# The second MLP projection's first 512 columns by seven block products in place of eight

## The chip, the cores and the metric

The kernel runs on one core of a Trainium2 chip. The metric is the device time of one execution in microseconds; what is compared is the median of several runs. The time before is 2069.7 us, the median of 3 runs (2069.42 to 2069.75).

## What is computed

A trunk of two layers on 256 tokens of width 2048. Each layer has a mixing half (RMSNorm, one input projection, attention heads and gated groups, an output projection, a residual add) and an MLP half. The change lies in the MLP, whose reference is:

```python
D_MODEL = 2048; SEQ = 256; DEPTH = 2
D_FF = 4 * D_MODEL
for l in range(DEPTH):
    ...
    h2 = rms_norm(x, norm2_g[l])
    x = x + jnp.square(jax.nn.relu(h2 @ w_up[l])) @ w_down[l]
return rms_norm(x, final_g)
```

## The kernel before

**Number format.** All weights and activations are float32. TensorE works in a reduced format (float32r), so each operand is split in two: ScalarE (ACT) writes the high part as a rounded copy (`hi` of a weight, L122), VectorE (DVE) writes the low part, the operand minus its high part (`lo`, L132). Every product is then three matmuls: high by high, high by low, low by high (L293, L295, L297). Activations are kept split in the same way: `hs` for the normed input, `half` for the hidden tensor (`to_half`, L494 to L496).

**Pieces of weight.** All weights stream through once, in pieces of 512 KB (class `Sub`: 128 partitions by 1024). One piece feeds one *step*. In a column-major step (`transposed`, L265) the piece holds 4 tiles of 128 rows by 256 columns; the weights are the stationary operand, and the 256 tokens move: 24 matmuls of 128x256. In a token-major step (`natural`, L300), used for parts of the input projection, 128 tokens are the stationary operand and 512 weight columns move. A piece has 6 buffers for the raw data, 7 for `hi` and 6 for `lo` (L47 to L49).

**The order.** It is written out by the last loop (L666 to L686), one step at a time: the `hi` of the piece five steps ahead, the `lo` of the piece four steps ahead, the DMA of the next raw piece, the step's matmuls, then what follows the step. Each engine takes its own instructions strictly in that order. Small jobs go through a queue (`later`, `run_queue`, L151 and L164): at the end of a step, jobs that are due are issued until a budget of 1.2 is used up (L52), each job with a written-down cost.

**The MLP.** The hidden width of 8192 is cut in eighths of 1024. The loop at L605 issues, for each eighth, 16 steps of `w_up` (four quarters of 256 hidden rows, four steps each), then 16 steps of `w_down` for the eighth before. After each quarter `after_up` (L594) scales the sums on DVE (L599), applies the squared ReLU on DVE (L600), and splits the result (ACT L495, DVE L496). After every second `w_down` step `update` (L351) adds 256 rows' sums into `x` (DVE L356). In the last eighth the update is final: in the first layer it is followed by the next layer's `hs` (ACT L193, DVE L197) and the squares for the norm (ACT L206, DVE L210), in the last layer by the squares and the gain (L206, L210, L214).

**PSUM.** Four banks (`acc`) serve the steps in turn, four (`aux`) the small matmuls.

## Time and profile before

| | |
|---|---|
| median of 3 runs | 2069.7 us |
| the profiled execution's own time | 2068.91 us |
| its span, first to last instruction | 2067.1 us |
| granted TensorE clock over the span | 0.998 |
| busy share of TensorE, VectorE, ScalarE | 99%, 61%, 45% |
| matmul instructions | 17242 |
| read from HBM | 390.65 MB, 190 GB/s over the span |

A row of the groups gives the line and engine, the operation, output and inputs, the shape, how often; then the busy time in all, the mean of one in ns, and the idle time of that engine just before. A row of the timeline gives start and length in us, and in square brackets how long the engine had been idle and what ended it. In the timeline a merged row (x4) runs from the start of the first to the end of the last. Matmuls overlap, so their spacing is read from their starts.

### The profile page before, as it was taken

The numbers are of one execution on the slowest core, as the hardware profiler recorded it, in microseconds if no ns is written. First come the engines' busy times: TensorE is split into PE (matmuls) and PEld (weight loads), VectorE is DVE, ScalarE is ACT, GpSimd is POOL, SyncE is SP. The second block draws the span as 40 slices with busy tenths as digits, with TensorE's granted clock in tenths as the row PEclk, the third lists the DMA queues.
The fourth block names the chain that finished last, engine by engine and source line by source line (L and its number), as shares of the span: only waits on it lengthen the run. The fifth ranks groups of instructions, "written<-read, shape, count | busy, mean of one in ns | idle before, by whom it ended". The sixth has DMA issues, their size and how long they took to land.

```text
span 2067.1 us, 40218 instructions
## 1 busy us (share of the span) xinstructions
PE 2054.5 (99%) x17242; PEld 2018.3 (98%) x17242; DVE 1253.6 (61%) x1494; ACT 933.0 (45%) x1135; POOL 67.8 (3%) x90
## 2 busy tenths in 40 slices
PE   9999999999999999999999999999999999999997
PEld 7998999999999999999989989999999999999997
DVE  7666766556555655655756666665565555555655
ACT  7555444344343443434545654543444434434434
POOL 0002300000000000000000032000000000000000
PEclk9999999999999999999999999999999999999999
DMA  8545555555555555555564455555655656555562
GB/s 318 183 164 178 189 192 183 197 202 186 189 200 201 187 188 198 201 188 201 186 216 160 169 186 181 194 182 204 204 184 184 204 194 200 190 192 196 187 201 91
DMA packets 112115, 395.37 MB, mean 191 GB/s; under 512 B 12352, under 2 KB 16448, under 8 KB 111936
## 3 DMA queue, kind: packets, MB, share of 16 engines
q1 hardware_dynamic: 110800, 389.86, 55.4%
q8 instruction: 135, 2.21, 0.4%
q10 hardware_dynamic: 1136, 2.94, 0.4%
q14 instruction: 44, 0.36, 0.1%
HBM read 390.65 MB, written 2.10 MB: 190 GB/s over the span
## 4 chain that ended last, share of the span: by engine, by line
PE 99%; DVE 0%; DMA 0%; ACT 0%; issue 0%; ACTq 0%; DVEq 0%
PE acc L293 29%; PE acc L297 29%; PE acc L295 29%; PE acc L316 3%; PE acc L318 3%; PE acc L317 3%; PE aux L541 0%; PE aux L443 0%; PE aux L485 0%; PE aux L472 0%; DVE x L696 0%; DMA x<-in_xT 0%; PE aux L446 0%; PE aux L487 0%; PE aux L384 0%; PE aux L221 0%
## 5 line engine op out<-in xcount | busy, mean ns | idle before, releaser
L122 ACT ACTIVATE hi<-raw 128x1024 fp32r<-128x1024 f32 (+1 forms) x741 | 755.6, 1049 | 453.3 <-PE acc L297 374.9
L132 DVE TENSOR_TENSOR lo<-raw,hi 128x1024 fp32r<-128x1024 f32 (+1 forms) x741 | 864.5, 1213 | 52.3 <-ACT hi L122 24.1
L293 PE MATMUL acc<-hs,hi 128*128 128x256 f32 x2816 | 779.8, 277 | 0.0
L297 PE MATMUL acc<-hs,hi 128*128 128x256 f32 x2816 | 777.4, 276 | 0.0
L295 PE MATMUL acc<-hs,lo 128*128 128x256 f32 x2816 | 777.4, 276 | 0.0
L293 PE MATMUL acc<-half,hi 128*128 128x256 f32 x2560 | 706.7, 276 | 0.0
L297 PE MATMUL acc<-half,hi 128*128 128x256 f32 x2560 | 706.6, 276 | 0.0
L295 PE MATMUL acc<-half,lo 128*128 128x256 f32 x2560 | 706.6, 276 | 0.0
L295 PEld LDWEIGHTS acc<-hs,lo 128*128 128x128 f32 x2816 | 528.7, 188 | 0.4 <-issue 0.2
L293 PEld LDWEIGHTS acc<-hs,hi 128*128 128x128 f32 x2816 | 528.6, 188 | 0.4 <-issue 0.2
L297 PEld LDWEIGHTS acc<-hs,hi 128*128 128x128 f32 x2816 | 528.5, 188 | 0.0
L295 PEld LDWEIGHTS acc<-half,lo 128*128 128x128 f32 x2560 | 480.5, 188 | 0.0
L293 PEld LDWEIGHTS acc<-half,hi 128*128 128x128 f32 x2560 | 480.5, 188 | 0.0
L297 PEld LDWEIGHTS acc<-half,hi 128*128 128x128 f32 x2560 | 480.5, 188 | 0.0
L356 DVE TENSOR_TENSOR x<-x,acc 128x512 f32<-128x512 f32 (+1 forms) x145 | 99.2, 684 | 318.8 <-PE acc L297 318.8
L495 ACT ACTIVATE half<-mz 128x512 fp32r<-128x512 f32 x64 | 40.6, 634 | 363.7 <-DVE mz L600 363.7
L599 DVE TENSOR_TENSOR mz<-acc,nR 128x512 f32<-128x512 f32 x64 | 44.3, 692 | 230.1 <-PE acc L297 230.1
L316 PE MATMUL acc<-hi,hs 128*128 128x512 f32 x256 | 101.6, 397 | 0.8 <-ACT hs L193 0.8
L318 PE MATMUL acc<-hi,hs 128*128 128x512 f32 x256 | 100.7, 393 | 0.0
L317 PE MATMUL acc<-lo,hs 128*128 128x512 f32 x256 | 99.9, 390 | 0.0
L193 ACT ACTIVATE hs<-x,cols 128x256 fp32r<-128x256 f32 x64 | 29.0, 501 | 96.0 <-DVE x L356 94.8
L496 DVE TENSOR_TENSOR half<-mz,half 128x512 fp32r<-128x512 f32 x64 | 44.3, 692 | 44.8 <-ACT half L495 44.8
(99 smaller groups left out, 688.8 us busy)
## 6 DMA issues: line engine op xcount, KB each, us to landing
raw<-in_w SPq DMA_DIRECT2D x731, 512.0 KB, 4.3
raw<-in_w SPq DMA_DIRECT2D x10, 256.0 KB, 5.3
x<-in_xT SPq DMA_DIRECT2D x7, 256.0 KB, 5.6
out<-x SPq DMA_DIRECT2D x7, 256.0 KB, 2.9
spb<-in_b_sp ACTq DMA_DIRECT2D x2, 512.0 KB, 8.2
wsp<-in_w_sp ACTq DMA_DIRECT2D x2, 512.0 KB, 9.7
con<-in_consts ACTq DMA_DIRECT2D x1, 512.0 KB, 7.5
x<-in_xT ACTq DMA_DIRECT2D x1, 256.0 KB, 4.2
```

The costliest lines, as they stand in the source:

```text
L122: act.activation(self.h[:, j * m:(j + 1) * m], self.raw[:, j * m:(j + 1) * m], AF.Copy)
L132: vec.tensor_tensor(lo[:, r], self.raw[:, r], self.h[:, r].bitcast(F32), op=OP.subtract)
L293: pe.matmul(o, lhsT=hi, rhs=xs[:, 0, :], start=(k0 + k == 0 and (two or cb == 0)), stop=False, skip_group_check=True)
L295: pe.matmul(o, lhsT=wt.lo[:, k, cb * P:(cb + 1) * P], rhs=xs[:, 0, :], start=False, stop=False, skip_group_check=True)
L297: pe.matmul(o, lhsT=hi, rhs=xs[:, 1, :], start=False, stop=last, skip_group_check=True)
L316: pe.matmul(ps, lhsT=xh, rhs=hi, start=(k0 + k == 0), stop=False)
L317: pe.matmul(ps, lhsT=xh, rhs=lo, start=False, stop=False)
L318: pe.matmul(ps, lhsT=xl, rhs=hi, start=False, stop=(k0 + k == KC - 1))
L356: vec.tensor_tensor(xj, xj, ps[j][:, 0:S] if alone else pair(ps)[:, j, :], op=OP.add)
L495: act.activation(t[:, c:c + 2, 0, :], src, AF.Copy)
L496: vec.tensor_tensor(t[:, c:c + 2, 1, :], src, t[:, c:c + 2, 0, :].bitcast(F32), op=OP.subtract)
L599: vec.tensor_tensor(z, pair(ps), n2.R[:, None, :].to_broadcast([P, 2, S]), op=OP.mult)
```

## The change

The first 512 of the 2048 columns of `w_down` (constant `FAST`) are computed by Strassen's scheme in Winograd's form. The hidden eighth A (256 tokens by 1024) is cut in 2 by 2 blocks, and so is the weight block B (1024 by 512). Seven products of blocks, with sums of blocks as operands, replace the eight of the plain method. The other 1536 columns are computed as before, by 12 steps per eighth.

**Product groups.** Per eighth there are two steps of a new kind (`fast`), called product groups below. Each covers 2 of the 4 tiles of 128 rows in each row half of B. Its 7 products have 2 row tiles each and 3 matmuls per tile: 42 matmuls of 128x256, with tokens stationary (from `half` or from the new tile of sums, `shared`) and weight columns moving. A product group takes four entries in the list of pieces: `Top` and `Bottom` are loaded; two `Sums` are made in place in the raw buffers by two DVE subtractions each, and then split like any piece. Of `Top` only the left half is split.

```diff
+    class Top(Sub):
+        def high(self, parts):
...
+            act.activation(self.hi, self.left(), AF.Copy)
+        def low(self, parts):
...
+            vec.tensor_tensor(self.lo, self.left(), self.hi.bitcast(F32), op=OP.subtract)
...
+    class Sums(Sub):
+        loads = False
...
+        def high(self, parts):
+            t, b = self.top, self.bottom
+            if self.second:
+                vec.tensor_tensor(b.right(), b.right(), t.left(), op=OP.subtract)
+                vec.tensor_tensor(b.left(), b.right(), b.left(), op=OP.subtract)
+            else:
+                vec.tensor_tensor(t.left(), t.right(), t.left(), op=OP.subtract)
+                vec.tensor_tensor(t.right(), b.right(), t.right(), op=OP.subtract)
+            self.raw = (b if self.second else t).raw
+            Sub.high(self, 1)
...
+                if first and p == 0:
+                    banks.extend(aux_bank() for _ in range(4))
+                half = tiles[0][0]
+                sums_ready()
+                extra = sum_parts[0]
...
+                for n, (a, lower_rows, tt, b, cols) in enumerate((
+                        (half, 0, 0, top, left), (half, 1, 0, bottom, left), (extra, 1, 0, bottom, right),
+                        (extra, 1, 1, upper, left), (extra, 0, 1, upper, right),
+                        (extra, 0, 0, lower, right), (half, 1, 1, lower, left))):
+                    o = banks[n // 2][:, n % 2 * 256:n % 2 * 256 + 256]
+                    for k in range(2):
+                        xh, xl = (a[:, 4 * lower_rows + 2 * p + k, i, tt * P:(tt + 1) * P] for i in range(2))
...
```

**Sums of the hidden tensor.** `after_up` now writes its result into one tile for the whole eighth (`inner`, part of `ar`). After the last quarter a queued job adds the blocks in place (`sums`, four DVE instructions), and four more queued jobs split them into `shared` (`parts`, one ACT and one DVE instruction each). A product group's matmuls are issued only after all four (`sums_ready`).

```diff
+                if c == 768:
+                    summed[0] = False
...
+                    later(1, 1.5, sums)
...
+        def sums():
+            a11, a12, a21, a22 = (inner[:, 4 * k:4 * k + 4, t * P:(t + 1) * P] for t in range(2) for k in range(2))
+            vec.tensor_tensor(a22, a21, a22, op=OP.add)
+            vec.tensor_tensor(a21, a11, a21, op=OP.subtract)
+            vec.tensor_tensor(a11, a22, a11, op=OP.subtract)
+            vec.tensor_tensor(a12, a12, a11, op=OP.subtract)
+            def parts(k):
+                to_half(sum_parts[0], k, inner[:, k:k + 2, :])
+                summed[0] = k == 6
+            for k in range(0, 8, 2):
+                later(0, 1.2, lambda k=k: parts(k))
```

**Sums over the eighths.** The seven products stay in the four `aux` banks over all eight eighths of a layer. After the last product group they are combined (`combine`: one ACT copy, seven DVE instructions of 128x256), turned back to column-major by eight TensorE transposes (`turn_back`), and added into `x` by two more updates.

```diff
+        def combine():
+            p1, p2, p3, p5, p7, p6, p4 = (banks[n // 2][:, n % 2 * 256:n % 2 * 256 + 256] for n in range(7))
+            b1, u, c11, c12, c21, c22 = (blocks[:, n, :] for n in range(6))
+            act.activation(b1, p1, AF.Copy)
+            vec.tensor_tensor(u, b1, p6, op=OP.add)
...
+            later(1, 1.5, lambda: turn_back(0, c11, c21))
+            later(1, 1.5, lambda: turn_back(2, c12, c22))
+        def turn_back(c, first, second):
+            ps = aux_bank()
+            for j in range(2):
+                for tt, src in enumerate((first, second)):
+                    o = j * S + tt * P
+                    pe.transpose(ps[:, o:o + P], src[:, j * P:(j + 1) * P], ident)
+            later(0, 1.5, lambda: update(n3, c, ps, True, last))
```

**Order of the steps.** The two product groups of an eighth stand among the 16 `w_up` steps of the next eighth (after the fourth and the eighth); after the last eighth's `w_up` they stand among its 12 `w_down` steps (after the third and the sixth).

```diff
+            rest = up or down
+            n = len(quick) + 1
+            for i in range(n):
+                steps.extend(rest[len(rest) * i // (n + 1):len(rest) * (i + 1) // (n + 1)] if quick else rest)
+                steps.extend(quick[i:i + 1])
```

**Memory and loads.** Ten small tiles of the mixing half, which had buffers of their own, become slices of two tiles (`shared`, `ar`), whose space serves the sums in the MLP. The DMA of a raw piece is issued as a buffer is counted free (`load_more`); a product group's two raw buffers are counted free when its two sums have been split.

Three places where instructions move are shown from the lists of instructions. First VectorE at the start of a layer's second eighth. `lo` is a weight's low part, `ar` the hidden tensor or its sums, `half` and `shared` the split tensors. Before, behind the last quarter of the first eighth:

```order
L599 TENSOR_TENSOR mz_4646<-acc_4531,nR_3856 128x512
L600 SCALAR_TENSOR_TENSOR mz_4646<-mz_4646 128x512
L496 TENSOR_TENSOR half_4393<-mz_4646,half_4393 128x2x256
L132 TENSOR_TENSOR lo_4653<-raw_4464,hi_4616 128x1024
L132 TENSOR_TENSOR lo_4684<-raw_4494,hi_4651 128x1024
L132 TENSOR_TENSOR lo_4714<-raw_4529,hi_4682 128x1024
L132 TENSOR_TENSOR lo_4744<-raw_4560,hi_4712 128x1024
```

Four low parts stood there for the four steps up to the next quarter. Now, behind the same quarter's L715, L716 and L612 (the former L599, L600, L496):

```order
L175 TENSOR_TENSOR lo_4225<-raw_4037,hi_4188 128x512
L729 TENSOR_TENSOR ar_78<-ar_78 128x4x128
L730 TENSOR_TENSOR ar_78<-ar_78 128x4x128
L731 TENSOR_TENSOR ar_78<-ar_78 128x4x128
L732 TENSOR_TENSOR ar_78<-ar_78 128x4x128
L205 TENSOR_TENSOR raw_4037<-raw_4037 128x2x256
L206 TENSOR_TENSOR raw_4037<-raw_4067,raw_4037 128x2x256
L162 TENSOR_TENSOR lo_4260<-raw_4067,hi_4223 128x1024
L612 TENSOR_TENSOR shared_4222<-ar_78,shared_4222 128x2x256
L202 TENSOR_TENSOR raw_4067<-raw_4067,raw_4037 128x2x256
L203 TENSOR_TENSOR raw_4067<-raw_4067 128x2x256
L162 TENSOR_TENSOR lo_4292<-raw_4037,hi_4258 128x1024
```

The sums of the hidden tensor (L729 to L732), the sums of weights (L205, L206, L202, L203) and the first split sum (L612 into `shared`) have come in between the low parts of the first product group. The same list goes on with:

```order
L612 TENSOR_TENSOR shared_4222<-ar_78,shared_4222 128x2x256
L162 TENSOR_TENSOR lo_4324<-raw_4067,hi_4290 128x1024
L715 TENSOR_TENSOR ar_78<-acc_4227,nR_3810 128x512
L716 SCALAR_TENSOR_TENSOR ar_78<-ar_78 128x512
L612 TENSOR_TENSOR half_4352<-ar_78,half_4352 128x2x256
L612 TENSOR_TENSOR shared_4222<-ar_78,shared_4222 128x2x256
```

The third split sum (the last row) stands behind the next quarter (L715, which waits for the fourth step's matmuls), and the fourth one low part further on. In the later eighths all four stand among the `w_down` steps that come first.

Second, TensorE in that first product group, from its second product on (`aux` are the banks of the products):

```order
L408 MATMUL aux_4365<-hi_4223,half_3842 128x256
L410 MATMUL aux_4365<-lo_4260,half_3842 128x256
L411 MATMUL aux_4365<-hi_4223,half_3842 128x256
L408 MATMUL aux_4366<-hi_4223,shared_4222 128x256
L410 MATMUL aux_4366<-lo_4260,shared_4222 128x256
L411 MATMUL aux_4366<-hi_4223,shared_4222 128x256
```

The third product is the first that reads the sums; with row half 1 it needs the third of the four split sums, the high part at L408 and the low part at L411.

Third, VectorE in the first layer's last eighth, behind the second product group: the low parts of the next pieces, then `combine`:

```order
L162 TENSOR_TENSOR lo_11686<-raw_11461,hi_11630 128x1024
L162 TENSOR_TENSOR lo_11688<-raw_11523,hi_11678 128x1024
L162 TENSOR_TENSOR lo_11690<-raw_11525,hi_11680 128x1024
L162 TENSOR_TENSOR lo_11692<-raw_11565,hi_11682 128x1024
L745 TENSOR_TENSOR ar_78<-ar_78,aux_4367 128x256
L746 TENSOR_TENSOR ar_78<-ar_78,aux_4365 128x256
L747 TENSOR_TENSOR ar_78<-ar_78,aux_4367 128x256
L748 TENSOR_TENSOR ar_78<-ar_78,aux_4366 128x256
L749 TENSOR_TENSOR ar_78<-ar_78,aux_4366 128x256
L750 TENSOR_TENSOR ar_78<-ar_78,aux_4368 128x256
L751 TENSOR_TENSOR ar_78<-ar_78,aux_4366 128x256
```

TensorE has two `w_down` steps between the second product group and the first four transposes; the transposes' first pair needs L746 and L750. All of this is new; before, only two low parts and an update stood there per two steps.

More of the change, by code (lines that the diff above doesn't have):

```diff
@@ L52 @@
 BUDGET = 1.2
+FAST = 512
 WARM = 11
@@ L263, in trunk, with sums_ready, collect @@
     steps = []
+    summed, sum_parts = [True], [None]
+    def sums_ready():
+        run_until(lambda: summed[0])
+    def collect(fn, *args, **kw):
+        n = len(steps)
+        fn(*args, **kw)
+        part = steps[n:]
+        del steps[n:]
+        return part
     def transposed(name, l, row0, nk, col0, ncols, moving, after, between=None, apart=False):
@@ L608, in layer @@
             if e:
-                transposed("w_down", l, (e - 1) * 1024, 8, 0, D, from_tiles([hid[e - 1]], NH),
-                           lambda c, ps, e=e: update(n3, c // P, ps, e == 8, last), apart=last and e == 8)
+                down = collect(transposed, "w_down", l, (e - 1) * 1024, 8, FAST, D - FAST, from_tiles([hid[e - 1]], NH),
+                               lambda c, ps, e=e: update(n3, (c + FAST) // P, ps, e == 8, last), apart=last and e == 8)
+                quick = collect(fast, "w_down", l, (e - 1) * 1024, 0, [hid[e - 1]], banks, e == 1, e == 8,
+                                lambda: later(1, 1.5, combine))
@@ L611, in layer @@
+            rest = up or down
[3 more added lines that the diff above has]
+                steps.extend(quick[i:i + 1])
+            if quick:
+                steps.extend(rest[len(rest) * n // (n + 1):])
+            if up:
+                steps.extend(down)
         if last:
@@ L624, in trunk, with load_more @@
         layer(l, norms[2 * l], norms[2 * l + 1], norms[2 * l + 2], l == DEPTH - 1)
-    subs = [wt for wt, _, _ in steps if wt is not None]
-    n_load, n_high, n_low = [0], [0], [0]
+    subs = [u for wt, _, _ in steps if wt is not None for u in (wt if isinstance(wt, tuple) else (wt,))]
+    n_load, n_high, n_low, n_raw = [0], [0], [0], [0]
     xv = xT.rearrange("(k p) t -> p k t", p=P)
-    def load_to(n, parts=1):
-        while n_load[0] < min(n, len(subs)):
+    def load_more():
+        while n_load[0] < len(subs):
+            if not subs[n_load[0]].loads:
+                n_load[0] += 1
+                continue
+            if n_raw[0] == RAW_BUFS:
+                return
             c = 2 * n_load[0]
@@ L636, in load_to @@
                 nc.sync.dma_start(x[:, c:c + 2, :], xv[:, c:c + 2, :])
-            subs[n_load[0]].load(parts)
+            subs[n_load[0]].load(2 if n_load[0] < HALVES else 1)
             n_load[0] += 1
+            n_raw[0] += 1
     def high_to(n, parts=1):
         while n_high[0] < min(n, len(subs)):
+            if not subs[n_high[0]].loads:
+                low_to(n_high[0] - 1)
             subs[n_high[0]].high(parts)
@@ L657, in trunk @@
         pe.matmul(spare[:, 0:P], lhsT=ones, rhs=ones, start=True, stop=True)
-    for i in range(RAW_BUFS):
-        load_to(i + 1, 2 if i < HALVES else 1)
+    load_more()
     for i in range(2):
@@ L663, in trunk @@
     n_high[0] = n_low[0] = 2
+    n_raw[0] -= 2
     done = 0
```

68 lines of the change are left out of this document (63 added, 5 removed).

## The prediction

> **What bounds the kernel now.** I read the engines' busy shares first, then the chain that ended last, then TensorE's own waits, and the mean over a stretch of MLP.
>
> ```profile
> PE 2054.5 (99%) x17242; PEld 2018.3 (98%) x17242; DVE 1253.6 (61%) x1494; ACT 933.0 (45%) x1135; POOL 67.8 (3%) x90
> PE 99%; DVE 0%; DMA 0%; ACT 0%; issue 0%; ACTq 0%; DVEq 0%
> PE aux L229 <- DVE nr L255: 1.2, 1, 1.2
> PE acc L316 <- ACT hs L193: 0.8, 1, 0.8
> 340.00:700.00 360.00, 360.00 (x3178) 360.00 (x3177) 212.13 (x226) 147.57 (x154) 0.00 (x0) 1.00 0.57 195
> ```
>
> TensorE runs without a gap: the chain is its own instructions, and its listed waits inside the run are about 1 us. In the MLP it starts 3178 matmuls in 360 us, one each 0.1133 us, at full clock. VectorE has 212 of 360 us of work there, DMA 57%. So a matmul less is 0.1133 us less, as long as VectorE's part is ready in time. VectorE goes in order, and its lead decides:
>
> ```profile
> 377.45 0.69 DVE L599 TENSOR_TENSOR mz<-acc,nR 128x512 f32<-128x512 f32 x1 [3.53 <-PE acc L297]
> 378.17 0.69 DVE L600 SCALAR_TENSOR_TENSOR mz<-mz 128x512 f32<-128x512 f32 x1
> 379.57 0.69 DVE L496 TENSOR_TENSOR half<-mz,half 128x512 fp32r<-128x512 f32 x1 [0.70 <-ACT half L495]
> 380.18 4.62 DVE L132 TENSOR_TENSOR lo<-raw,hi 128x1024 fp32r<-128x1024 f32 x4
> 388.33 0.69 DVE L599 TENSOR_TENSOR mz<-acc,nR 128x512 f32<-128x512 f32 x1 [3.53 <-PE acc L297]
> 378.90 0.64 ACT L495 ACTIVATE half<-mz 128x512 fp32r<-128x512 f32 x1 [5.78 <-DVE mz L600]
> 379.44 2.94 ACT L122 ACTIVATE hi<-raw 128x1024 fp32r<-128x1024 f32 x3
> ```
>
> Four steps of 24 matmuls take 10.88 us (377.45 to 388.33). VectorE works 2.73 us on a quarter and then 1.13 us from one low part to the next ((4.62-1.22)/3), and is idle for the last 3.53 us. What follows another in a chain of results starts 0.72 us later, what doesn't, 0.61 us (379.57 to 380.18). ACT's split starts 0.73 us behind L600's start.
>
> **What TensorE saves.** Per eighth and layer the 512 columns took 4 blocks of 128 columns x 8 row tiles x 3 = 96 matmuls; now 2 groups x 42 = 84. Over 16 eighths: 192 fewer, 192 x 0.1133 = 21.8 us. That the new ones have the same price (moving weights, stationary tokens) is taken from token-major steps, at 0.23 us for 512 columns:
>
> ```profile
> 1034.85 0.39 PE L316 MATMUL acc<-hi,hs 128*128 128x512 f32 x1
> 1035.08 0.39 PE L317 MATMUL acc<-lo,hs 128*128 128x512 f32 x1
> 1142.21 0.66 PE aux L472 x6
> ```
>
> The 16 transposes cost 0.11 us each (0.66/6), 1.8 us. TensorE's own balance is **-20.0 us**.
>
> **VectorE in the ordinary product group.** Prices:
>
> ```profile
> L132 DVE TENSOR_TENSOR lo<-raw,hi 128x1024 fp32r<-128x1024 f32 x731 | 858.0, 1220 | 48.7 <-ACT hi L122 20.5 <-issue 16.3 <-PE acc L317 9.1
> L132 DVE TENSOR_TENSOR lo<-raw,hi 128x512 fp32r<-128x512 f32 x10 | 6.5, 687 | 3.7 <-ACT hi L122 3.6
> L426 DVE TENSOR_TENSOR q<-q,sw 128x512 f32<-128x512 f32 x8 | 5.5, 692 | 0.3
> L412 DVE TENSOR_TENSOR cosR<-con,aux 128x256 f32<-128x256 f32 x2 | 0.8, 420 | 6.0 <-ACT nR L234 6.0
> raw<-in_w SPq DMA_DIRECT2D x731, 512.0 KB, 4.3
> ```
>
> A block sum of 512 elements from SBUF is L426's 0.69 us; runs of 256 cost nothing more, since L496 writes such runs in 0.69. Between the quarters around a group VectorE has the quarter (2.73), four low parts of ordinary steps (4.53), and for the next group the short low part (0.61), four subtractions (2.9) and three low parts (3.4): 14.2 us, against 4.76 + 10.88 = 15.6 us of TensorE. So it fits, with 1.4 us to spare. The nearest deadline is the low part for the step behind a group: done 2.73+1.22 = 3.95 us after the quarter's end, needed after 42 x 0.1133 = 4.76. I put these 30 groups at nothing; the cover is 0.6 to 0.8 us each. DMA isn't late: a raw buffer is filled in 4.3 us (the last row) and split again some four steps, 10.9 us, after it came free; the bytes stay the same, so the 57% hardly moves.
>
> **The first product group of each layer is different.** There is no `w_down` phase behind the first eighth, so the sums meet the group four steps later. I add up the order shown above from L599's start, t=0. Quarter 2.73; short low part 0.61; four sums 4 x 0.72; two subtractions 1.44; low part 1.13: 8.8. The first split sum waits for ACT, which first writes the new `hi` (from 7.66, 0.98 to its next start) and then the split's high part (0.63): 9.3, and 0.61 on VectorE: 9.9. Two subtractions: 11.4. ACT again 0.98+0.63: 13.0, the second split sum to 13.6, low part 14.7. Only now comes L715, which was ready at 10.88: VectorE is 3.9 us late. L715 and L716 1.44, ACT's two splits, L612 to 17.5, the third split sum's low part to **18.2**. TensorE starts the group at 10.7 (0.2 us ahead of t=10.88, as the first two rows below stand to the third) and needs that part at its 15th matmul, at 12.3. It waits **5.9 us**, in both layers: 11.8 us. Lower bound: if VectorE were not late, quarter plus split, 2.73+0.69 after 10.88, less the 1.4 us of work in front of it: 2.0 us. Upper: every one of the 8 block sums at a low part's 1.22 in place of 0.69 gives 4 more, 10 us. I take 5.9, since L426 is the same operation.
>
> ```profile
> 1029.93 0.28 PE L297 MATMUL acc<-half,hi 128*128 128x256 f32 x1
> 1030.05 0.39 PE L316 MATMUL acc<-hi,hs 128*128 128x512 f32 x1
> 1030.25 0.69 DVE L356 TENSOR_TENSOR x<-x,acc 128x512 f32<-128x512 f32 x1 [0.29 <-PE acc L297]
> 1031.51 0.89 DVE L197 SCALAR_TENSOR_TENSOR hs<-x,cols,hs 128x256 fp32r<-128x256 f32 x2 [0.58 <-ACT hs L193]
> 1032.43 0.69 DVE L210 TENSOR_TENSOR nacc<-nacc,nsq 128x512 f32<-128x512 f32 x1
> 1033.04 4.62 DVE L132 TENSOR_TENSOR lo<-raw,hi 128x1024 fp32r<-128x1024 f32 x4
> 2049.95 0.69 DVE L210 TENSOR_TENSOR nacc<-nacc,nsq 128x512 f32<-128x512 f32 x1 [0.70 <-ACT nsq L206]
> ```
>
> **The clock behind such a wait.** At the end of the run TensorE falls idle, and the granted clock follows 1.3 us later; at its start the same 128x128 matmuls take 0.19 us each in place of 0.11:
>
> ```profile
> 2057.50:2058.00 0.50, 0.06 (x1) 0.00 (x0) 0.40 (x2) 0.00 (x0) 0.00 (x0) 1.00 0.00 0
> 2058.50:2059.00 0.50, 0.00 (x0) 0.00 (x0) 0.50 (x2) 0.00 (x0) 0.00 (x0) 0.87 0.14 51
> 2059.00:2059.50 0.50, 0.00 (x0) 0.00 (x0) 0.50 (x2) 0.00 (x0) 0.00 (x0) 0.50 0.80 273
> 1.05 4.14 PE L657 MATMUL aux<-ones 128*128 128x128 f32 x22 [1.05 <-DVE warm L653]
> 2056.85 0.71 PE L229 MATMUL aux<-con,nr 128*128 128x128 f32 x4 [1.21 <-DVE nr L255]
> ```
>
> 22 matmuls in 3.9 us from first to last start: 13 at 0.22 and 9 at 0.11, about 2.9 us at half speed, a loss of 1.5 us. I charge 1.5 per long wait, **3.0 us**; bounds 0 (no drop) and 3.4 each. The Trainium skill ("TensorE: Matmul & The Clock Gate", "What's actually happening") has the drop after an idle window of about 3.4 us and full clock after as long a busy one, which would be 1.7 us a wait and 0.4 us more in all, and no drop at the shorter waits below; the end rows, with a drop 1.3 us after the last matmul, don't show where its window began.
>
> **The last eighth.** An update with what follows now occupies VectorE for 2.79 us in the first layer (1030.25 to 1033.04) and 2.0 in the last (0.69, the L210 row's idle 0.70, 0.61). With three steps, a group, three steps, a group, VectorE's list in order (first layer) is: update, two subtractions, low part, two subtractions, low part: 5.8; update 7.8; four low parts 12.3; short low part, subtractions, low part 15.5; update from 15.6 (TensorE) to 18.4; subtractions and two low parts 22.2; update 25.0; the low part for the step behind the second group 26.2. TensorE is there at 25.7: wait 0.5. Then four low parts (30.6) and `combine`, whose sixth sum ends 2.5 us later (0.42 each, L412): 33.1, while the transposes are reached at 31.6: wait 1.5. They now end so late that the next layer's first `hs` come with 0.2 us of wait: 2.2 in all. In the last layer the shorter updates leave 0.3 at the transposes, and two updates (`turn_back`'s) that delay the last one by 0.8: 1.1. Together **3.3 us**; bounds 1 (VectorE 2 us earlier) and 6.
>
> **Sum.** -20.0 + 11.8 + 3.0 + 3.3 = -1.9 us. Against the profiled execution, 2068.9 us, that is 2067.0; the median of the runs lies 0.8 above it, so 2067.8 us. Within 0.2% (4.1 us) is what I call the same, about what a measurement of this kernel tells from no change.
>
> **Rivals.**
>
> *The first group's wait is short.* If VectorE is not late there, 2.0 us a layer and no drop of the clock: -20.0 + 4.0 + 3.3 = -12.7, 2057 us. For it: VectorE had 3.5 us idle per quarter. Against: the list adds 4 sums, 4 subtractions and 2 splits in the same 10.9 us.
>
> *VectorE late at every group (slower).* It decides once the 14.2 us pass 15.6 by more than the 0.7 us cover of the low part behind a group: 2.1 us more per group. If each of its five strided instructions took 1.2 in place of 0.69 us (a low part's price), 2.6 us more, TensorE would wait 0.5 us in 14 second groups, 7 us, and the two first groups 4 us longer, 8 us: 2083 us. Against it: L496's 0.69 with runs.
>
> *The clock gate is quicker and longer (slower).* If a wait of 1.5 us is enough, and the half speed lasts 6 us: 3 us at each first group and at one transposes' wait, 9 in place of 3.0: 2074 us. For it: the drop 1.3 us after the last matmul. Against: TensorE had already idled 1.21 us shortly before (the last of those rows), with the clock still full.
>
> *TensorE saves nothing,* because the new matmuls cost more: a wait-free group would take over 5.4 us. The 512-column rows speak against it.
>
> **Chances.** Forecast 0.54; short wait 0.23; VectorE late 0.08; clock 0.10; no saving 0.05. The forecast's own range is 2061 to 2076 (waits of 5 to 7 us, clock 0 to 3.4 each, last eighth 1 to 6); of its 0.54, 0.11 lie below 2065.6 and 0.07 above 2073.8, 0.36 between. So faster 0.23 + 0.11 = 0.34, same 0.36, slower 0.08 + 0.10 + 0.05 + 0.07 = 0.30. The range reaches to the short wait below and past the clock case above, and leaves out the two other slower ones: 2057 to 2077.
>
> **What would show it.** TensorE's waits: one of 5 to 7 us before L411 in each layer's second eighth, and a granted clock below 1 behind it; no waits of TensorE in the third to eighth eighths, which get 12 x 0.1133 = 1.4 us shorter each; about 1.5 us at L760 in the first layer. Waits of 0.5 us and more behind every second group would make it wrong upwards, a first group without a wait downwards.

## The result, and the profile after

| | before | after |
|---|---|---|
| median of 4 runs | 2069.72 us | 2093.10 us |
| lowest and highest | 2069.42, 2069.99 | 2092.52, 2094.38 |
| the profiled execution's own time | 2068.91 us | 2093.35 us |
| its span | 2067.1 us | 2091.5 us |

The change made the kernel slower: ratio 1.0114, 95% interval 1.0096 to 1.0131. The forecast was 2067.8 us, its range 2057 to 2077. In the page of the profile after, the rows of the busy times and of the chain that ended last:

```profile
PE 2066.8 (99%) x17066; PEld 2028.3 (97%) x17066; DVE 1464.4 (70%) x1800; ACT 1008.9 (48%) x1265; POOL 68.7 (3%) x90
PE 31%; DVE 0%; ACT 0%; issue 0%; DVEq 0%
```

TensorE has 176 matmuls fewer and is busy 12 us longer, still 99% of the span. The chain is still TensorE alone; followed back, it reaches to 1423.72 us, where the second of the two long waits ends. Of TensorE's waits in the run after, by what they waited for (us in total, times, longest), two that the run before has as well are left out:

```profile
PE aux L408 <- ACT shared L611: 10.4, 2, 5.2
PE aux L760 <- DVE ar L750: 1.1, 1, 1.1
PE aux L297 <- DVE nacc L286: 0.7, 1, 0.7
PE acc L431 <- ACT hs L269: 0.5, 1, 0.5
```

The last one lies at 6.05 us, at the program's first step, where the run before has 0.8 us.

**The two long waits** are where the forecast had them. Rows picked from the timeline of VectorE, then from that of TensorE, in the first layer's second eighth:

```profile
377.53 0.69 DVE L715 TENSOR_TENSOR ar<-acc,nR 128x512 f32<-128x512 f32 x1 [3.53 <-PE acc L384]
392.26 0.68 DVE L715 TENSOR_TENSOR ar<-acc,nR 128x512 f32<-128x512 f32 x1
394.98 0.68 DVE L612 TENSOR_TENSOR shared<-ar,shared 128x512 fp32r<-128x512 f32 x1
```

```profile
389.46 0.28 PE L411 MATMUL aux<-hi,half 128*128 128x256 f32 x1
394.91 0.58 PE L408 MATMUL aux<-hi,shared 128*128 128x256 f32 x1 [5.17 <-ACT shared L611]
395.29 0.41 PE L410 MATMUL aux<-lo,shared 128*128 128x256 f32 x1
395.71 0.58 PE L411 MATMUL aux<-hi,shared 128*128 128x256 f32 x1
...
400.57 0.37 PE L408 MATMUL aux<-hi,half 128*128 128x256 f32 x1
400.78 0.29 PE L410 MATMUL aux<-lo,half 128*128 128x256 f32 x1
```

The third split sum starts 17.45 us after L715's first start; the forecast's order gave 17.5. TensorE stands for 5.45 us from start to start ahead of its 13th matmul, which needs the sum's high part (L611 on ACT). The 15th, L411, needs the low part and starts as L612 ends (394.98 + 0.68): at 395.71, 5.9 us later than it would without a wait (388.21, the group's first start, and 14 x 0.1133). From 396.09 on the starts lie 0.213 us apart until 400.57. The windows of the run after around it (PEclk is the number behind POOL's):

```profile
390.00:392.00 2.00, 0.00 (x0) 0.00 (x0) 1.48 (x2) 1.43 (x2) 0.00 (x0) 1.00 0.37 125
392.00:394.00 2.00, 0.00 (x0) 0.00 (x0) 1.64 (x3) 0.29 (x1) 0.00 (x0) 0.98 0.67 201
394.00:396.00 2.00, 1.08 (x3) 0.79 (x4) 1.63 (x3) 2.00 (x4) 0.00 (x0) 0.50 0.53 199
400.00:402.00 2.00, 2.00 (x16) 2.00 (x16) 1.97 (x3) 0.64 (x1) 0.00 (x0) 0.81 0.91 332
```

The clock halves at about 393.9 (0.98 is a drop for the last 4% of that window) and is back at about 400.8 (0.81: half for 38% of it), 6.8 us later; in layer 2 it is down from 1421.3 to 1428.2, as long, but more of that lies inside the wait. The group takes 13.16 us from its first start to the next step's (401.37) in place of 42 x 0.1133 = 4.76, and 12.53 us in layer 2 (1417.02 to 1429.55). So 8.40 and 7.77 us are lost, 16.2 together: 5.9 of each is the wait up to the 15th matmul, and the 2.5 and 1.9 behind it are the clock.

**The part that wasn't foreseen** needs no wait and shows no lower clock. The windows of the run after over two stretches of 60 us without a long wait, one in each layer, then the same windows of the run before:

```profile
420.00:480.00 60.00, 60.00 (x532) 60.00 (x531) 43.15 (x49) 26.36 (x29) 0.00 (x0) 1.00 0.60 203
1450.00:1510.00 60.00, 60.00 (x512) 60.00 (x511) 40.75 (x47) 25.37 (x28) 0.00 (x0) 1.00 0.56 191
```

```profile
420.00:480.00 60.00, 60.00 (x532) 60.00 (x531) 34.38 (x36) 24.75 (x25) 0.00 (x0) 1.00 0.55 187
1450.00:1510.00 60.00, 60.00 (x532) 60.00 (x531) 32.66 (x33) 22.63 (x22) 0.00 (x0) 1.00 0.62 206
```

(A count has the two or three matmuls in it that are under way at the edges.) Layer 1 matches the kernel before; layer 2 makes 20 matmuls fewer in 60 us at a granted clock of 1.00, with TensorE busy throughout. The timeline shows the place where it changes, at the end of a group of the third eighth:

```profile
573.65 0.28 PE L408 MATMUL aux<-hi,half 128*128 128x256 f32 x1
573.77 0.28 PE L410 MATMUL aux<-lo,half 128*128 128x256 f32 x1
573.88 0.28 PE L411 MATMUL aux<-hi,half 128*128 128x256 f32 x1
574.00 0.28 PE L380 MATMUL acc<-hs,hi 128*128 128x256 f32 x1
574.11 0.28 PE L382 MATMUL acc<-hs,lo 128*128 128x256 f32 x1
574.23 0.28 PE L384 MATMUL acc<-hs,hi 128*128 128x256 f32 x1
574.35 0.28 PE L380 MATMUL acc<-hs,hi 128*128 128x256 f32 x1
574.47 0.28 PE L382 MATMUL acc<-hs,lo 128*128 128x256 f32 x1
574.59 0.28 PE L384 MATMUL acc<-hs,hi 128*128 128x256 f32 x1
```

0.113 us apart up to 574.11, 0.12 apart from there on. TensorE has two pitches for the same matmul: 113.3 ns and, on the mean of all of them, 117.8 ns. The slow one lasts until the end of the eighth's second group, and the same happens in each later eighth of layer 1. In layer 2 it is the other way round: slow from the second group to the end of the next eighth's first group, three quarters of the time. I call a 128x256 matmul slow when the next one starts 115.5 to 119.5 ns after it, and count them over each layer's MLP from its third step on. What they take beyond 113.3 ns is 24.3 us after, 0.2 us before. (The expectations below counted from 373 us on, some 20 fewer a layer.)

| kernel | slow matmuls, MLP of layer 1, layer 2 | beyond 113.3 ns |
|---|---|---|
| before | 23, 24 of 6096 | 0.2 us |
| after | 1101, 4377 of 6000 | 24.3 us |
| probe | 5358 of 6208, 3941 of 6398 | 41.4 us |
| pad2 | 4358, 4391 of 6032 | 38.9 us |
| late | 1098, 1096 of 6000 | 9.7 us |
| padlate | 1113, 1114 of 6032 | 9.9 us |
| turn12 | 4333 of 6000, 1120 of 6012 | 24.2 us |
| adjacent | 5323, 3784 of 6000 | 40.5 us |
| near1 | 1104, 530 of 6000 | 7.3 us |
| near2 | 742, 759 of 6000 | 6.7 us |
| best, best2 | 761, 761 and 759, 760 of 6000 | 6.8, 6.7 us |
| reset | 5446, 5429 of 6000 | 48.4 us |
| latereset | 5345, 5343 of 6000 | 47.5 us |
| latereset4 | 60, 127 of 6000 | 0.8 us |
| one32 | 5583, 5583 of 6096 | 49.6 us |
| two32 | 25, 26 of 6096 | 0.2 us |

So the span's 24.4 us come together from -20.0 (fewer matmuls), +16.2 (two first groups), +24.1 (slow pitch, against before) and a rest of 4.1. Of the rest, 1.7 lie in layer 1's MLP (1.1 are the wait at L760), 0.4 in layer 2's, 1.7 behind TensorE's last `w_down` matmul (15.1 us to the end for 13.4 before) and 0.3 elsewhere. (The expectations below take 16.8 for the first groups, twice layer 1's loss.)

### The profile page after: what moved, and what is told of

It is laid out like the page before. It is cut to its first block, busy times and chain, and to the rows that moved or that the text cites. A ratio compares the mean times of both kernels' runs of the same rounds, so it can differ in the third digit from the quotient of the medians.

```text
span 2091.5 us, 40406 instructions
## 1 busy us (share of the span) xinstructions
PE 2066.8 (99%) x17066; PEld 2028.3 (97%) x17066; DVE 1464.4 (70%) x1800; ACT 1008.9 (48%) x1265; POOL 68.7 (3%) x90
## 5 line engine op out<-in xcount | busy, mean ns | idle before, releaser
L152 ACT ACTIVATE hi<-raw 128x1024 fp32r<-128x1024 f32 (+1 forms) x773 | 783.7, 1046 | 420.8 <-PE acc L384 194.5
L162 DVE TENSOR_TENSOR lo<-raw,hi 128x1024 fp32r<-128x1024 f32 (+1 forms) x773 | 907.8, 1211 | 42.0 <-ACT hi L152 25.8
L380 PE MATMUL acc<-half,hi 128*128 128x256 f32 x2048 | 569.5, 278 | 0.0
L382 PE MATMUL acc<-half,lo 128*128 128x256 f32 x2048 | 569.1, 278 | 0.0
L384 PE MATMUL acc<-half,hi 128*128 128x256 f32 x2048 | 569.0, 278 | 0.0
L380 PEld LDWEIGHTS acc<-half,hi 128*128 128x128 f32 x2048 | 387.6, 189 | 0.0
L382 PEld LDWEIGHTS acc<-half,lo 128*128 128x128 f32 x2048 | 384.4, 188 | 0.1
L384 PEld LDWEIGHTS acc<-half,hi 128*128 128x128 f32 x2048 | 384.4, 188 | 0.0
L611 ACT ACTIVATE half<-ar 128x512 fp32r<-128x512 f32 x72 | 45.6, 633 | 323.5 <-DVE ar L716 308.9
L715 DVE TENSOR_TENSOR ar<-acc,nR 128x512 f32<-128x512 f32 x64 | 44.2, 691 | 196.0 <-PE acc L384 196.0
L612 DVE TENSOR_TENSOR half<-ar,half 128x512 fp32r<-128x512 f32 x72 | 49.8, 692 | 50.3 <-ACT half L611 50.3
L408 PE MATMUL aux<-hi,shared 128*128 128x256 f32 x256 | 73.4, 287 | 10.4 <-ACT shared L611 10.4
```

The source lines that it names most:

```text
L152: act.activation(self.h[:, j * m:(j + 1) * m], self.raw[:, j * m:(j + 1) * m], AF.Copy)
L162: vec.tensor_tensor(lo[:, r], self.raw[:, r], self.h[:, r].bitcast(F32), op=OP.subtract)
L380: pe.matmul(o, lhsT=hi, rhs=xs[:, 0, :], start=(k0 + k == 0 and (two or cb == 0)), stop=False, skip_group_check=True)
L382: pe.matmul(o, lhsT=wt.lo[:, k, cb * P:(cb + 1) * P], rhs=xs[:, 0, :], start=False, stop=False, skip_group_check=True)
L384: pe.matmul(o, lhsT=hi, rhs=xs[:, 1, :], start=False, stop=last, skip_group_check=True)
L408: pe.matmul(o, lhsT=xh, rhs=hi, start=(first and p == 0 and k == 0 and n % 2 == 0), stop=False, skip_group_check=True)
```

## The experiments

Medians of before on the same chips lay between 2069.47 and 2069.60 us in all of them.

**What turns the pitch: probe, pad2, late, padlate.** Three theories. *Count*: a group's 42 matmuls are no multiple of 4, as those of all other steps are. *Boundary*: stationary tokens followed by stationary weights turn it over. *Load*: the additional work of the other engines slows TensorE's reads. probe puts matmuls into the kernel before, the other three edit the changed kernel.

```diff
 # probe: in transposed, behind a step's matmuls
+                if name in ("w_up", "w_down") and count:
+                    spare = aux_bank()
+                    for i in range(count):
+                        xs, b = moving(k0 + i % 4), wt.lo if i % 3 == 1 else wt.hi
+                        pe.matmul(spare[:, 0:256], lhsT=b[:, i % 4, 0:P] if kind == "w" else xs[:, 0, 0:P],
+                                  rhs=xs[:, 0, :] if kind == "w" else b[:, i % 4, :], ...)
 # pad2: in fast, behind a group's products
+                for i in range(2):
+                    pe.matmul(banks[3][:, 256:512], lhsT=xh, rhs=hi, start=False, ...)
 # late: where the groups stand (padlate: both)
+            cuts = [len(rest) * (i + (2 if e == 1 else 1)) // 4 for i in range(2)] if quick else []
```

> The kernel before, no Strassen, with extra matmuls of the common shape (128 x 128 by 128 x 256, float32r, into a bank nobody reads) put into single steps: in layer 1 after the eighth up step of eighths 2 to 8 with stationary weights as the steps around them, 1, 1, 1, 1, 2, 2, 6 of them, and in the down steps with stationary tokens 1, 3, 2, 6, then with stationary weights 42, 42, 2; in layer 2 in the up steps with stationary tokens 2, 4, 6, 12, 42, 42, 44, and in the down steps weights 3, 3, tokens 24, 48, weights 6, 24, tokens 42. Theory count: TensorE has two pitches, 113.3 ns and 117.8 ns, and a number of matmuls that is no multiple of 4 changes from one to the other: the pitch of the steps behind turns over after 2, 6 and 42, whoever is stationary, and not after 4, 12, 24, 44 and 48. Theory boundary: it turns over wherever stationary tokens are followed by stationary weights: after every insert with tokens, whatever its number, and after none with weights. Theory load: the slower pitch comes from what VectorE, ScalarE and the transfers do beside the groups: nothing turns over here, 113.3 ns throughout, and the time is 2069.7 + 414 x 0.1133 = 2116.6 us.

> The changed kernel with 2 more matmuls of the same shape at the end of each of the 32 product groups (44 for 42, into the unread half of the fourth bank). Theory count: the slow pitch is gone but for what the two long waits leave: 2093.1 + 32 x 2 x 0.1133 (7.3) - 24.1 = 2076.3 us. Theory boundary: the pitch turns over behind every group as before: 2093.1 + 7.3 = 2100.4 us. Theory load: the same 2100.4 us.

> The changed kernel with the two groups of the first eighth of each layer put behind 8 and 12 of the up steps for 4 and 8, so that the third split sum (17.5 us behind the last step's L715) is there before the group starts (21.6 us). All theories: the wait of 5.3 us and the 3.1 us of half clock behind it go, in both layers: 2093.1 - 16.8 = 2076.3 us. If the long wait of layer 2 is also what put its long stretches into the slow pitch (layer 1 has 4.8 us of it, layer 2 19.5 us), layer 2 comes down to layer 1's 4.8 us: 2061.6 us.

> Both edits: 44 matmuls in each group, and the first eighth's groups behind 8 and 12 up steps. Theory count: 2093.1 - 16.8 - 24.1 + 7.3 = 2059.5 us. Theories boundary and load: 2083.6 us, or 2068.9 us if the long wait is what put layer 2 into the slow pitch.

probe, one run of 2159.04 us, read from its trace insert by insert (pitch ahead of it, pitch behind it):

| inserted | fast to slow | slow to fast | stayed |
|---|---|---|---|
| stationary weights, 1, 1, 1, 1, 2, 2, 6, 42, 42, 2, 3, 3, 6, 24 | | | all 14 (12 slow, 2 fast) |
| stationary tokens | 1, 2, 24, 48, 42, 42 | 6, 12, 42, 44 | 3, 2, 6, 4 (all slow) |

Load is out: the pitch turns in a kernel without sums. Count is out: 42 with stationary weights turn nothing, and 12, 24, 44 and 48 with tokens do. Boundary holds for every insert that met the fast pitch; from the slow one four short inserts of the eight changed nothing (2, 3, 4, and one of two with 6). Over all traces of this study, of 223 groups or inserts of 42 with tokens, weights right behind them and no wait of 1 us in them, 220 turned the pitch. The time agrees within 1.5 us: 2069.6 + 46.9 (414 matmuls more) + 41.1 (slow pitch) = 2157.6 us.

pad2: 2107.53 us, but its four runs are 2100.15, 2100.58, 2114.48, 2115.89, on two levels. The lower one is what boundary expected (2100.4). In the profiled one (2114.48) layer 1 is mostly slow as well, though in after it wasn't. late: **2062.55 us** (2062.10 to 2063.12), ratio 0.9966, interval 0.9953 to 0.9979: the long waits gone, and layer 2 like layer 1, as the second figure of the expectation had it. TensorE's waits in late start with

```profile
PE aux L305 <- DVE nr L331: 1.2, 1, 1.2
```

and hold none at L408. padlate: 2069.65 us, 7.1 above late, which is the price of its 64 matmuls (7.3); count's 2059.5 is out a second time.

**Which way round: turn12, adjacent, near1, near2.** turn12 adds 12 matmuls with stationary tokens at one place of layer 2 of the changed kernel. The other three move the groups in late: `first` is 8 steps in the first eighth where groups stand, else a quarter of the steps.

```diff
 # turn12: in transposed, at one step
+                if (l, name, col0, n) == (1, "w_up", 1024, 13):
+                    for i in range(12):
+                        xs = moving(k0 + i % 4)
+                        pe.matmul(BANKS[1][3][:, 256:512], lhsT=xs[:, 0, 0:P], rhs=(wt.lo if i % 3 == 1 else wt.hi)[:, i % 4, :], ...)
 # adjacent: 0, near1: 1, near2: 2
+            cuts = [first, first + 2] if quick else []
```

> The changed kernel with 12 more matmuls at one place: in layer 2, behind the 14th up step of the second eighth, with stationary tokens (into the unread half of the fourth bank). Theory boundary (stationary tokens followed by stationary weights turn the pitch over, whatever the number): from there on layer 2 runs its long stretches at 113.3 ns as layer 1 does, so its slow matmuls fall from 4378 to about 1200: 2093.1 + 12 x 0.1133 (1.4) - 14.1 = 2080.4 us. A theory in which the pitch is set by the load or the place in the program: 2094.5 us.

> The kernel with the first eighth's groups late, and the two groups of every eighth with no step between them (84 matmuls, then up steps). Theory boundary: one turn per eighth in place of two, so every second eighth is slow from group to group, 756 matmuls x 4.44 ns = 3.4 us, 8 of them: 2062.55 - 9.6 + 26.9 = 2079.9 us, more where VectorE can't follow with the block sums of both groups. Theory count (84 is a multiple of 4): no slow stretch at all, 2053 us.

> The same with one step between the two groups of an eighth in place of four (three in the last eighth). Theory boundary: slow are only the step between and the second group, 66 matmuls for 138 (114 in the last eighth): 1104 fewer slow matmuls x 4.44 ns = 4.9 us, 2057.6 us. If VectorE can't make the second group's block sums in that time, each of the 16 eighths loses what it is late by, and 0.3 us at each is enough to eat the gain (2062.5 us or more).

> The same with two steps between the two groups. Theory boundary: 720 fewer slow matmuls, 3.2 us: 2059.4 us. If VectorE is late for the second group, less late than with one step between.

turn12: median 2094.19 us, four runs at 2080.29, 2092.99, 2095.40, 2108.37. The lowest is the expected time, the others lie some 14 and 28 us above it. The profiled one (2095.40) says why, in its windows:

```profile
420.00:480.00 60.00, 60.00 (x512) 60.00 (x511) 41.25 (x47) 25.30 (x28) 0.00 (x0) 1.00 0.57 200
1450.00:1510.00 60.00, 60.00 (x526) 60.00 (x525) 40.29 (x45) 27.97 (x32) 0.00 (x0) 1.00 0.57 198
```

Layer 2 did turn over (1120 slow matmuls for 4377), but now layer 1 is slow, and up to the insert its matmuls stand in the same order as in after. So the program alone doesn't set how a layer goes on behind a long wait; the levels say that it differs from run to run, and from there on the groups only turn it over. In the four traces with such waits (after, pad2, turn12, reset) TensorE came out of all eight at the slow pitch. Where no float32 matmul stands at that group's end, the end turned it to the fast one five times of six; layer 1 of after is the sixth. Why is open. late, which has no long wait, has runs within 1.0 us; after, pad2 and turn12 have two such waits, and pad2's runs spread over 15.7 us, turn12's over 28.1. That all four runs of after lie within 1.9 us, with one layer slow in the profiled one, would then be chance; the other three were not traced, so that isn't shown.

adjacent: 2109.33 us, 2091.93 to 2124.71; the traced run is the slowest. Boundary's 2079.9 is missed for two reasons. VectorE can't feed two groups in a row, as the first of TensorE's waits shows:

```profile
PE aux L410 <- DVE lo L162: 18.8, 28, 1.1
```

And there are 9107 slow matmuls where boundary has 8 x 756 = 6048. In 14 of the 16 pairs VectorE holds TensorE up, and 9 of these leave the slow pitch as it was; the two pairs without a wait turn it. So boundary is shown for undisturbed groups alone. Count's "no slow stretch" isn't borne out either, but with waits inside the pairs this tests it less than pad2 and padlate do.

near1: 2071.72 us, 2065.41 to 2082.40. In the fastest run, which is the traced one, VectorE is late at L410 by 0.5 us twice, and 12 more of the second groups are held up there by some 0.14 us (0.26 us from start to start for 0.118). Layer 2 has the expected half of late's slow matmuls (530). Layer 1 has 1104, because at one of the short hold-ups (916.61 us) the pitch turns inside the group, whose end then turns it back to slow for the long stretch behind. So a hold-up of 0.14 us can turn the pitch, here once of 12; that this makes the spread of the runs is only argued. near2: 2063.40 us for 2059.4. The slow matmuls fell as expected (1501 for late's 2194, 3.1 us), and the gain went into waits:

```profile
PE aux L760 <- DVE ar L750: 2.4, 2, 1.2
PE aux L760 <- DVE ar L746: 2.0, 2, 1.2
```

In the last eighth there is more VectorE work behind each step, and a second group that comes a step earlier brings the transposes forward while VectorE is still busy.

**Setting the pitch, and the version that wins: reset, latereset, best, best2.** The trace lists a float32 matmul as two instructions, called passes here. In the traces so far the norm's four passes at L305, between two steps, had always left the fast pitch; reset tries to get that with one float32 matmul, two passes.

```diff
 # reset (on after), latereset (on late): in fast, behind a group's products
+                pe.matmul(banks[3][:, 256:384], lhsT=ident, rhs=ident, start=False, ...)
 # best (on late)
+            cuts = [first, first + (2 if up else 3)] if quick else []
 # best2: best, and in combine
-            later(1, 1.5, lambda: turn_back(0, c11, c21))
-            later(1, 1.5, lambda: turn_back(2, c12, c22))
+            later(2, 1.5, lambda: turn_back(0, c11, c21))
+            later(2, 1.5, lambda: turn_back(2, c12, c22))
```

> The changed kernel with one float32 matmul of 128 x 128 by 128 x 128 (two passes, into the unread half of the fourth bank) behind each of the 32 product groups. In the traces so far the float32 matmuls of 128 columns that stand between steps (L305, 4 passes) have 113.3 ns behind them 20 times of 20, though the step ahead ran at 117.8 ns. Theory boundary, with such a matmul setting the faster pitch: nothing is slow behind a group, whatever the two long waits leave: 2093.1 - 24.1 + 32 x 0.23 (7.5, from L305's rows) = 2076.5 us, and the runs agree within about 1 us. If the matmul sets nothing: 2100.6 us, with runs some 14 us apart where a long wait turned a layer's pitch over.

> The same float32 matmul behind each group, and the first eighth's groups behind 8 and 12 up steps. If it sets the faster pitch: 2062.55 - 9.6 + 7.5 = 2060.5 us, no slow matmul in the MLP. If it sets nothing: 2070.1 us.

> The first eighth's groups late, two steps between the groups of an eighth, but the last eighth as in the kernel called late (three steps, then three). Theory boundary: 14 x 48 fewer slow matmuls x 4.44 ns = 3.0 us below 2062.55: 2059.6 us. In near2 the same saving was there (slow matmuls 1455 for 2152 in the MLPs) and went into waits at L760 of the last eighths (4.4 us for 1.0) and the half clock behind them. If VectorE is late elsewhere too: 2062.5 us.

> best, with the transposes L760 one step later behind the eight block operations L745 to L751 (two steps for one). The wait of 1.0 us at L760 in layer 1 goes: 2058.6 us. If the transposes' delay only moves the wait to the last update and the next layer's first step: 2059.6 us or more.

The float32 matmul does set the pitch, but to the slow one: reset 2123.90 us, latereset 2106.29 us, with slow pitch behind all 64 groups of the two traces. It was slow ahead of the matmul 62 times, where the group's end alone would have turned it to fast, and fast twice. My expectation fell on the sign; the point that it sets something stands, and both kernels' runs now agree within 1.2 us, reset's in spite of its two long waits.

**best: 2059.38 us** (2059.31 to 2059.66, 5 runs), ratio to before 0.9951, interval 0.9938 to 0.9965. It was expected at 2059.6 and beats both kernels. best2: 2067.82 us for 2058.6. The wait at L760 went, and what came in its place is the second case of the expectation, larger than I had it:

```profile
PE acc L431 <- ACT hs L269: 4.7, 2, 3.6
PE aux L297 <- DVE nacc L286: 3.0, 1, 3.0
```

The last update now comes so late that the next layer's first step waits for `hs`, and the last norm for the squares.

**The state by itself: one32, two32, latereset4.** Two passes had left the slow pitch 64 times, the four passes of L305 (two matmuls) the fast one 20 times of 20. The first two put one or two float32 matmuls per layer into the kernel before.

```diff
 # one32: range(1), two32: range(2), in transposed of the kernel before
+                if (name, col0, n) == ("w_up", 1024, 7):
+                    spare = aux_bank()
+                    for i in range(1):
+                        pe.matmul(spare[:, i * P:(i + 1) * P], lhsT=ident, rhs=ident, start=(i == 0), ...)
 # latereset4: latereset with two matmuls, 256 + i * P
```

> The kernel before with one float32 matmul of 128 x 128 by 128 x 128 (2 passes, a bank nobody reads) in each layer, behind the eighth up step of the second eighth; 2 matmuls in the whole program, some 0.25 us each. If the pitch is a lasting state and 2 passes set the slow one, as behind the groups: all that follows in the MLP of that layer, some 5300 matmuls a layer, runs at 117.8 ns: 2069.5 + 0.5 + 2 x 5300 x 4.44 ns (47.1) = 2117 us. If the slow pitch needs stationary tokens ahead of it or the load of the block sums: 2070.0 us.

> The same with two such matmuls (4 passes) at each of the two places. If the number of passes decides, 4 leave the fast pitch: 2069.5 + 2 x 0.46 = 2070.4 us. If any float32 matmul between steps sets the slow one: 2117.5 us.

> The changed kernel with the first eighth's groups late and 4 float32 passes behind each group for 2. If 4 passes set the fast pitch whatever stood ahead: 2062.55 - 9.6 + 32 x 0.46 (14.7) = 2067.7 us and no slow matmul in the MLP. If what decides is that they follow stationary tokens: some 2106.3 + 7.2 = 2113.5 us.

one32: 2119.45 us (2119.28 to 2119.69), ratio 1.0242, interval 1.0227 to 1.0257. Two matmuls in the whole program cost 50 us. Its timeline at the first of them (L301, two passes):

```profile
398.99 0.28 PE L293 MATMUL acc<-hs,hi 128*128 128x256 f32 x1
399.11 0.28 PE L295 MATMUL acc<-hs,lo 128*128 128x256 f32 x1
399.22 0.28 PE L297 MATMUL acc<-hs,hi 128*128 128x256 f32 x1
399.34 0.38 PE L301 MATMUL aux<-con 128*128 128x128 f32 x2
399.48 0.36 PE L293 MATMUL acc<-hs,hi 128*128 128x256 f32 x1
399.68 0.28 PE L295 MATMUL acc<-hs,lo 128*128 128x256 f32 x1
399.80 0.28 PE L297 MATMUL acc<-hs,hi 128*128 128x256 f32 x1
```

and one and the same window of 360 us in one32, then in two32:

```profile
500.00:860.00 360.00, 360.00 (x3059) 360.00 (x3058) 200.97 (x208) 140.63 (x144) 0.00 (x0) 1.00 0.55 186
```

```profile
500.00:860.00 360.00, 360.00 (x3179) 360.00 (x3178) 208.56 (x217) 146.33 (x151) 0.00 (x0) 1.00 0.56 194
```

Nothing waits, the clock is granted in full, the engines have less to do per microsecond, and TensorE makes 120 matmuls fewer. two32: 2070.34 us, 0.85 over before (expected 0.9). latereset4: 2067.53 us (expected 2067.7), fast behind all 32 groups. So the state needs nothing of the change, it lasts until the next such event, and one float32 matmul of 128 columns between steps (two passes) leaves the slow one, whatever stood ahead. In latereset4 and two32 the pitch was fast ahead as well, so they show only that four passes keep it; that four passes turn slow to fast is shown by the norm's rows alone (L305, L229 in before: 34 times of 34 in the 17 traces).

**What stays open:** what the two states are in the hardware, and why these events turn or set them. No rule by count covers the cases: the eight passes of one column at L297 left the slow pitch 34 times of 34, the six transposes of L588 never, the four transposes of L760 three times of 50. The inserts with tokens swap the two operands' roles together, so the runs don't tell whether the stationary or the moving one matters. And why a group whose matmuls were held up sometimes fails to turn the pitch isn't known.

## Why the prediction was wrong

**The failed step** is "I put these 30 groups at nothing", with what it rests on: "That the new ones have the same price (moving weights, stationary tokens) is taken from token-major steps". The new matmuls do have the old price, 113.3 ns where the pitch is fast (573.65 to 574.00). But a group changes the price of all the matmuls behind it, those of the unchanged steps too, until the next group: 24.1 of the some 26 us between the profiled run's 2093.35 and the 2067.0 forecast for it. (The clock is 1.4 of what is left, the last eighths and the end some 0.8.) The size is partly luck: one layer was mostly slow in that run, and by turn12's runs it could have been none or both, some 14 us less or more. The rival "TensorE saves nothing" looked for a dearer group, which isn't there, and held the rest of the MLP fixed. I took 0.1133 us from one mean over 360 us as a constant of the machine. The trace of before had the other value in plain sight, in the timeline behind the norm's eight passes (L221), for one step of 24 matmuls:

```profile
337.71 0.95 PE L221 MATMUL aux<-ones,nacc 128*128 128x1 f32 x8
...
339.07 0.28 PE L295 MATMUL acc<-hs,lo 128*128 128x256 f32 x1
339.19 0.28 PE L297 MATMUL acc<-hs,hi 128*128 128x256 f32 x1
339.31 0.28 PE L293 MATMUL acc<-hs,hi 128*128 128x256 f32 x1
339.42 0.28 PE L295 MATMUL acc<-hs,lo 128*128 128x256 f32 x1
...
341.43 0.61 PE L229 MATMUL aux<-con,nr 128*128 128x128 f32 x4
```

The other steps, one by one:

- *TensorE's own balance, -20.0.* Right. late has it: 2069.6 - 20.0 + 9.5 (slow pitch against before) + 3.5 (last eighths and end, from late's own trace) = 2062.6 for 2062.55.
- *VectorE in time at the ordinary groups.* Right. After has no wait at one of them, though VectorE is busy 43 of 60 us. The cover was as thin as stated: with one step between the groups (near1) it is late, with none (adjacent) by 18.8 us.
- *The first group's wait, 5.9 us.* 5.9 at the 15th matmul, in both layers: right in mechanism and size. It shows as two waits, most of it at the 13th for the high part. That its place was right is shown by late, where the groups stand 10.9 us further back and no wait is left.
- *The clock behind it, 1.5 us each.* Mis-sized: 2.5 and 1.9, inside the bounds of 0 and 3.4. I had taken the 2.9 us of half speed from the start of the run; here the clock was down for 6.8 us, and 5.0 and 3.6 us of that lay behind the 15th matmul. The Trainium skill ("TensorE: Matmul & The Clock Gate", "What's actually happening") has a free-running window of 3413 ns; 6.8 us agrees with two of these, and in pad2's first layer the clock was down for 3.4 us, which agrees with one. The forecast's estimate of 1.7 us a wait, by one window, was short in after for the same reason as my 1.5.
- *The last eighth, 3.3 us.* 4.1 as the rest of the sum: 1.7 for 2.2 in the first layer, with 1.1 us at L760 (1.5 forecast) and no wait at the next layer's first step (0.2); 2.1 for 1.1 in the last, most of it behind TensorE's last `w_down` matmul; and 0.3 elsewhere.
- *What would show it.* The long waits came at L408 and L411, and 1.1 us at L760. Eighths 1.4 us shorter each didn't come: in layer 1 they are 0.7 us shorter (86.3 us between first groups, for 768 x 0.1133 = 87.0), since 138 matmuls of each are slow; in layer 2 they are 1.4 us longer (88.4).

## What to carry to other kernels

When TensorE is the bound, take its pitch from the starts in the timeline in several places, ahead of and behind each kind of interruption, and count matmuls in equal windows: a lasting change of 4% showed here as neither a wait nor a lower clock, and 99% busy hid it. An edit that adds a kind of boundary to TensorE's stream (another stationary operand, a small float32 matmul) has to be priced with the pitch of all that follows, and a cheap probe in the kernel before, a few matmuls into an unused bank, prices it ahead of the edit. A stall of TensorE cost three things here: the wait, half the clock, and a pitch behind it that the program alone no longer determines; move the consumer behind its producer by the worked-out lag before tuning anything finer.

## What the runs showed of the hardware that I had not expected

- Back-to-back 128x256 float32r matmuls, each with its own weight load, run at 113.3 or 117.8 ns a matmul at granted clock 1.00, and keep their pitch for hundreds of microseconds (one32: some 5560 slow ones on end in each layer).
- Stationary tokens followed by stationary weights turned the pitch over 220 times of 223; the reverse change kept it 312 times of 312. (Both counts leave out groups with a wait of 1 us in them.) One float32 matmul of 128 columns (two passes) left the slow pitch 66 times of 66 (64 in reset and latereset, 2 in one32), two of them (four passes) kept the fast one 34 of 34 (32 in latereset4, 2 in two32), and the norm's four passes turned slow to fast 34 of 34.
- With two long waits and the clock halved behind them, executions of the same instructions differed in steps of some 14 us (turn12: 2080, 2093, 2095, 2108), which is one layer's long stretches at the slow pitch; one execution of each kernel was traced.
- A hold-up of 0.14 us turned the pitch once of 12 (near1).
- The Trainium skill ("TensorE: Matmul & The Clock Gate", "Wait — 56ns, not 53.3ns?") gives back-to-back matmuls N columns at 2.4 GHz plus about 2.5 ns, measured at N of 128 and 512; for 256 that is 109.2 ns, my estimate from the page's figures. The rows here, float32r with a weight load each, don't agree: both pitches lie above it.
